# A float32 decoder layer on one core: the weight buffers moved to many residues modulo 256 bytes

## The chip, the cores and the metric

The kernel runs on one core of one Trainium2 chip. The metric is device time in microseconds (us), from launch to end, of the whole layer; lower is better. The core has a TensorE (PE: matmuls, with a separate record, PEld, for loading the stationary operand), a VectorE (DVE), a ScalarE (ACT), a GpSimd (POOL) and a SyncE (SP, which here only starts transfers). Its on-chip memory, SBUF, has 128 partitions; a tile takes the same range of bytes in each of them. "Address" below means that byte offset within a partition.

## The reference

One decoder layer over 512 tokens of width 1024, batch 1, in float32:

```python
x = x + 0.5 * swiglu(rms_norm(x, ffn1_norm), ffn1_gate, ffn1_up, ffn1_down)   # hidden width 2816
z = rms_norm(x, mix_norm) @ w_in                  # seven groups of 512 columns
y = concat(hgrn2_recurrence(z[0:4]), gated_short_convolution(z[4:7]))
x = x + y @ w_out
q = rms_norm(x, xattn_norm) @ w_q_mem             # 4 heads of 256
k, v = split(rms_norm(mem, mem_norm) @ w_kv_mem)  # 256 memory rows
x = x + softmax(q k^T / 16) v @ w_o_mem
x = x + 0.5 * swiglu(rms_norm(x, ffn2_norm), ffn2_gate, ffn2_up, ffn2_down)
out = rms_norm(x, final_norm)
```

## The kernel before

Features lie on partitions and tokens along the free axis, in 8 tiles of 128 features by 512 tokens, until the last projection, which puts tokens on partitions. To get float32 products out of TensorE's shorter format (float32r), every operand is split into a high and a low part of 12 bits each. A product then takes three matmuls, by `mm3`: high weight by high activation, high weight by low activation, low weight by high activation. Each loads 128x128 stationary values (512 bytes in each partition) and streams the other operand past them (512 columns, 2,048 bytes in each partition, nearly everywhere). There are 4,576 such float32r matmuls with 512 columns, 290 with 256, and 223 plain float32 ones.

Weights come in units of 128x1024 values. `weight_steps` gives a unit a tile `raw` (where the transfer lands), a tile `whi` and a tile `wlo`. ScalarE writes `whi` from `raw`, VectorE writes `wlo = raw - whi`, and TensorE then reads both in 24 matmuls. The pool `wpool` has three buffers each of `raw`, `whi` and `wlo`, used in turn. In the two feed-forward halves `extra[0]` names a pool with a fourth pair, used by each unit whose number is 3 modulo 4. The order of the work is the order of the code on each engine; a tile's next writer waits until its last reader is done.

Who is stationary differs. In the hidden layers, the first down projection, the mixer's projections, the queries, the memory's keys and the output projections, the weights are stationary and activations are streamed (`mm3`). In the values of the recurrence (`psv`), the memory's values (`psvm`) and the last down projection (`pso`), activations are stationary and weights are streamed.

The program's pools lay tiles one behind another, so each tile's address follows from the sizes ahead of it. In the built program before, the residues of the addresses modulo 256 are:

| tiles | residue |
|---|---|
| `x` (`xall`), its split tiles (`x_f1..`, `x_mx..`, `x_xa..`, `x_f2..`, `at..`), `raw`, all three `whi`, all three `wlo` | 160 |
| the fourth `whi` and `wlo`; the hidden activations `a_f1..`, `a_f2..`; everything in the mixer's pool (`qkh`, `kb`, `y..`, `memh`, `kh`, `q..`, `vh`, `pt..`) | 32 |
| `ones_r`, a matrix of ones | 224 |

All slices within these tiles start at multiples of 256 bytes. Take the distance of a pair as the address of the stationary operand being loaded, less that of the operand being streamed meanwhile, modulo 256. Of the 4,575 neighbouring pairs with 512 streamed columns, 2,927 have distance 0, 1,631 have distance 128, and 17 (with `ones_r` and the like) have 64 or 192. Distance 128 comes from a fourth unit against `x` tiles, or an ordinary unit against hidden activations or the mixer's tiles.

The stages in the profiled execution, by their first matmul: first hidden layer 6.3 us, first down projection 250.7 us, mixer 372.9 us, its output projection 557.7 us, memory's keys 603.7 us, output of the attention 719.6 us, last down projection 1009.1 us.

Of the kernel before, what the change touches and what calls it, by code (L numbers as in the profile page):

```python
# [8 lines left out]
F32 = mybir.dt.float32  # L9
F32R = mybir.dt.float32r  # L10
# [9 lines left out]
FF = 2816  # L20
KT = D // P          # 8 feature tiles
FT = FF // P         # 22 hidden tiles
NH = 4               # recurrence heads
TT = S // P          # 4 token tiles
MT = MEM // P        # 2 memory token tiles
MH = 4               # memory attention heads
EPS = 1e-6
# [3 lines left out]

# columns of the packed per-feature vectors
V_FFN1, V_MIX, V_XATT, V_MEM, V_FFN2, V_FIN = 0, 8, 16, 24, 32, 40
# [5 lines left out]
def decoder_layer(ctx: ExitStack, tc: tile.TileContext, xT, memT, vecs, masks, ident_d,  # L39
# [3 lines left out]
    xpool = ctx.enter_context(tc.tile_pool(name="xpool", bufs=KT))  # L43
    wpool = ctx.enter_context(tc.tile_pool(name="wpool", bufs=3))
    tmp = ctx.enter_context(tc.tile_pool(name="tmp", bufs=2))
    sm = ctx.enter_context(tc.tile_pool(name="sm", bufs=2))
# [7 lines left out]

    # ---------------------------------------------------------------- inputs
    inv_d = const.tile([P, 1], F32, name="inv_d")
# [7 lines left out]

    # the tensor engine's clock rises, and the activation tables come, while the first loads
    # are under way
    early = const.tile([P, 1], F32, name="early")
# [8 lines left out]
    msk = const.tile([P, len(LEVELS), 2, 64], U8, name="msk")  # L76
    lbv = const.tile([P, 2, NH], F32, name="lbv")
    xall = xpool.tile([P, KT, S], F32, tag="x", name="xall", bufs=1)
    x = [xall[:, k] for k in range(KT)]

    # ---------------------------------------------------------------- helpers
    n_unit = [0]
    extra = [None]          # a pool with room for a fourth block

    def weights(src, shape):
        """A block of weights, split into two parts of 12 bits each."""
        raw, hi, lo, load, split = weight_steps(src, shape)
        load(0, shape[0])
        split(0, shape[0])
        return hi, lo  # L90

    def weight_steps(src, shape):
        n = n_unit[0]
        n_unit[0] += 1
        raw = wpool.tile([P, 1024], F32, tag="raw", name=f"raw{n}")
        more = extra[0] is not None and n % 4 == 3
        hi, lo = (extra[0].tile([P, 1024], F32R, tag="x" + t, name=f"{t}{n}", bufs=1) if more else
                  wpool.tile([P, 1024], F32R, tag=t, name=f"{t}{n}") for t in ("whi", "wlo"))
        a, b = shape
        w = a * b  # L100

        def load(k0, k1, queue=nc.sync):
            queue.dma_start(raw[:, k0 * b:k1 * b], src[:, k0 * b:k1 * b])

        def split(k0, k1):
            c = slice(k0 * b, k1 * b)
            nc.scalar.activation(hi[:, c], raw[:, c], AF.Copy)  # L107
            nc.vector.tensor_tensor(lo[:, c], raw[:, c], r32(hi[:, c]), ALU.subtract)  # L108

        v = lambda t: t[:, :w].rearrange("p (a b) -> p a b", b=b)  # L110
        return raw, v(hi), v(lo), load, split

    def mm3(out, wh, wl, xh, xl, first, last):
        """out += (wh + wl).T @ (xh + xl), but for the product of the two low parts'
        2**-24."""
        nc.tensor.matmul(out, lhsT=wh, rhs=xh, start=first, stop=False)  # L116
        nc.tensor.matmul(out, lhsT=wh, rhs=xl, start=False, stop=False)  # L117
        nc.tensor.matmul(out, lhsT=wl, rhs=xh, start=False, stop=last)  # L118
# [6 lines left out]
    class Norm:  # L125
        """Sums of squares over features, tile by tile; then 1/rms by token in both layouts."""

# [12 lines left out]
        def tokens(self):  # L140
# [8 lines left out]
            nc.gpsimd.tensor_tensor(rst, rs, mhalf[:, :nt], ALU.pow)  # L149
            # 1/rms on a diagonal, in two parts of 12 bits: a sum over it fills all partitions  # L150
            hi = sm.tile([P, nt], F32R, tag="rsh", name=f"rsh_{self.name}")
# [23 lines left out]
    def prepare(gcol, name):  # L175
        """Scaled inputs of the next projections, from x's tiles."""
        norm = Norm(name, S)
        out = []

        def tile_done(k):  # L180
            hi, lo = new_split("x", xpool, f"x_{name}{k}")
            split_x(x[k], gcol + k, hi, lo)
            norm.add(x[k])
            out.append((hi, lo))

        return norm, out, tile_done
# [3 lines left out]

    # ---------------------------------------------------------------- SwiGLU halves
    def ffn_hidden(name, hp, xs, norm, wgu, first):
# [36 lines left out]

    # ---------------------------------------------------------------- first half  # L230
    norm, xs, _ = prepare(V_FFN1, "f1")
# [54 lines left out]

    # ---------------------------------------------------------------- mixer
    norm_a, xs_a, done_a = prepare(V_XATT, "xa")
    with tc.tile_pool(name="mix", bufs=8, reuse_waits="tile") as mp:
# [9 lines left out]

        # lower bound of the forget gate: the softmax over the two rows, its first row  # L300
        mx = sm.tile([P, NH], F32, tag="lb0", name="lbmx")
# [40 lines left out]

        # values, tokens on partitions
        v = mp.tile([P, TT, 512], F32, tag="b", name="v")
# [30 lines left out]
        def conv_u(j):  # L375
# [12 lines left out]
            for d in (1, 2):  # L388
# [3 lines left out]
                for n in range(d):  # L392
                    # steps at the edge between tiles: 2m -> 2m + 1, and 1 -> 2
                    tap(i, yt[:, :, 1, P - 1 - n:P - n], ut[:, :, 0, P - d + n:P - d + n + 1])
# [12 lines left out]

        # projections that keep the tensor engine busy between the steps of the recurrence
        fill = []
# [7 lines left out]

        # scores of the recurrence: s on partitions, t along the row; pairs within a tile of
        # 128 steps by halving, each pair through the step between its halves
        kmix = mp.tile([P, 2, 2 * NH, P], F32, tag="b", name="kmix")  # L420
# [8 lines left out]

        def pairs(a):            # [P, heads x tile pairs, tile of the pair, step]  # L430
            return a.rearrange("p n (m r t) -> p (n m) r t", r=2, t=P)
# [5 lines left out]
        kp, qp = pairs(kb), pairs(qa)  # L437
        tot, off = f, 0          # products of f over blocks of h steps: [P, heads, S // h]
        for li, h in enumerate(LEVELS):
            nb = P // (2 * h)  # L440
            # earlier halves of the first tile's blocks beside those of the second's, whose
            # steps run backwards
            km = kmix[:, li % 2]
# [3 lines left out]
            for half in range(2):  # L447
                ps = bank(f"ps_l{h}_{half}")
                for n in range(4):
                    g = 4 * half + n  # L450
                    # later halves of the first tile's blocks, then of the second's
                    qs = pick(qp[:, g], h, (P - h, 2), (2 * h, nb), (1, h))
                    nc.tensor.matmul(ps[:, n * P:(n + 1) * P], lhsT=km[:, g], rhs=qs, start=True, stop=True)
                pv = ps.rearrange("p (g r b c) -> p g r b c", g=4, r=2, c=h)
                for r in range(2):
# [3 lines left out]
                        pv[:, :, r])  # L459
            # blocks of 2h steps  # L460
            nb2 = S // (2 * h)
# [11 lines left out]
            filler(2 if li < 4 else 1)  # L473
        # tiles 0 -> 1 and 2 -> 3 of 128 steps
        so1 = mp.tile([P, NH, 2, P], F32, tag="b", name="so1")
# [13 lines left out]
        filler(2)  # L489
        # the first 256 steps -> the last 256  # L490
        so2 = mp.tile([P, NH, 2, 256], F32, tag="b", name="so2")
# [37 lines left out]
        for hh in range(NH):  # L529
# [9 lines left out]
            ys[hh] = (hi, lo)  # L539
        # the memory, split like x; its norm  # L540
        norm_k = Norm("mem", MEM)
# [27 lines left out]

        # ------------------------------------------------------------ attention to the memory  # L570
        norm_2, xs_2, done_2 = prepare(V_FFN2, "f2")
# [133 lines left out]

    # ---------------------------------------------------------------- second half, last norm
    with tc.tile_pool(name="hid2", bufs=FT, reuse_waits="tile") as hp:
        extra[0] = hp
        hid = ffn_hidden("f2", hp, xs_2, norm_2, w2, None)
        # from here on tokens lie on partitions  # L710
        for k in range(KT):
# [24 lines left out]
        def finish_tile(i):  # L736
# [11 lines left out]
            nc.vector.scalar_tensor_tensor(rs, ss[:, :1], EPS, ss[:, 1:], op0=ALU.add, op1=ALU.add)  # L748
            rst = sm.tile([P, 1], F32, tag="rstf", name=f"rstf{i}")
            nc.gpsimd.tensor_tensor(rst, rs, mhalf[:, :1], ALU.pow)  # L750
            return y, rst

        def store_tile(i, y, rst):
            # two engines share the products with 1/rms and the gain
            a, b = (1, 0) if i < TT - 1 else (0, 1)
# [21 lines left out]
def _tokens():  # L777
    """The order of the tokens on chip: every second tile of 128 from its end."""
    import numpy as np
# [5 lines left out]
def _layout(i):  # L785
# [3 lines left out]

    def cols(w, kt):       # [K, M] -> [M / 128, 128, K / 128 * 128]: lhsT blocks by output tile  # L790
        k, m = w.shape
# [55 lines left out]
```

## Time and profile before

| | |
|---|---|
| median of 2 runs | 1141.56 us (1141.05 to 1142.07) |
| span of the profiled execution, first to last instruction | 1138.9 us |
| TensorE busy | 1129.7 us |
| weight loads busy (beside the matmuls) | 937.9 us |
| VectorE busy | 572.6 us |
| ScalarE busy | 391.2 us |
| mean traffic to and from memory | 98 GB/s |

The profiled execution's time is given as its span alone; the median of the runs is 2.7 us above that, and what lies around the span (launch and end) is the same code in both kernels. A matmul's recorded duration (about 390 ns) is longer than the time from its start to the next one's start, because matmuls are pipelined: two are always under way. So durations of matmuls say little here; the time between starts is what adds up to the span.

### The profile page before, as it was taken

How to read it: one execution, taken by the hardware profiler on the slowest of the kernel's cores; microseconds unless marked ns; L12 is line 12 of the kernel's file. 1: busy time of each engine (PE TensorE's matmuls, PEld its weight loads, DVE VectorE, ACT ScalarE, POOL GpSimd, SP SyncE). 2: the span in 40 equal slices, each digit the busy share in tenths (PEclk: the TensorE clock that was granted, in tenths of full speed). 3: DMA queues.
4: the chain of work that ended last, by engine and by line, in shares of the span. 5: the costliest groups of instructions: out<-in, count | busy, mean ns of one | idle time of the engine just before them, and what ended most of it. 6: DMA issues, size and time to landing. Idle time of an engine off the chain costs nothing. (4 is left out here: it accounts for less than half of the span.)

```text
span 1138.9 us, 12928 instructions
## 1 busy us (share of the span) xinstructions
PE 1129.7 (99%) x5232; PEld 937.9 (82%) x5232; DVE 572.6 (50%) x829; ACT 391.2 (34%) x542; POOL 18.1 (2%) x21
## 2 busy tenths in 40 slices
PE   9999999999999999999999999999999999999997
PEld 7888888888888888888889888888888888888885
DVE  6644444443333466885677566464544444432224
ACT  6423332222222344324455346343323223331123
POOL 0000000000000000000100000000000000000002
PEclk9999999999999999999999999999999999999999
DMA  6333222332332222222134323223222232232211
GB/s 232 121 104 99 93 93 93 102 91 86 101 92 102 74 93 84 84 74 93 56 129 138 122 75 129 64 92 123 93 93 93 96 107 94 93 102 101 93 56 74
DMA packets 33195, 112.02 MB, mean 98 GB/s; under 512 B 3968, under 2 KB 4736, under 8 KB 33136
## 3 DMA queue, kind: packets, MB, share of 16 engines
q1 hardware_dynamic: 30960, 108.02, 28.9%
q10 hardware_dynamic: 2016, 2.66, 0.7%
q8 instruction: 41, 0.67, 0.2%
q0 software_dynamic: 160, 0.52, 0.1%
q14 instruction: 18, 0.15, 0.0%
HBM read 109.09 MB, written 2.10 MB: 98 GB/s over the span
## 5 line engine op out<-in xcount | busy, mean ns | idle before, releaser
L107 ACT ACTIVATE whi<-raw 128x1024 fp32r<-128x1024 f32 (+4 forms) x208 | 213.0, 1028 | 632.9 <-PE ps_f L117 277.7
L108 DVE TENSOR_TENSOR wlo<-raw,whi 128x1024 fp32r<-128x1024 f32 (+4 forms) x208 | 245.1, 1182 | 194.7 <-ACT whi L107 194.4
L210 DVE TENSOR_TENSOR u_f<-ps_f,rsb_f 128x512 f32<-128x512 f32 x44 | 30.4, 690 | 128.6 <-PE ps_f L118 128.6
L207 DVE TENSOR_TENSOR t_f<-ps_f,rsb_f 128x512 f32<-128x512 f32 x44 | 30.4, 690 | 79.4 <-PE ps_f L118 79.4
L211 DVE TENSOR_TENSOR u_f<-u_f,t_f 128x512 f32<-128x512 f32 x44 | 30.3, 692 | 4.0
L208 ACT ACTIVATE t_f<-t_f 128x512 f32<-128x512 f32 x44 | 27.7, 630 | 1.6 <-DVE t_f L207 1.1
L116 PE MATMUL psk<-memh,whi 128*128 128x256 f32 x64 | 18.1, 283 | 0.0
L117 PE MATMUL psk<-meml,whi 128*128 128x256 f32 x64 | 18.0, 281 | 0.0
L118 PE MATMUL psk<-memh,wlo 128*128 128x256 f32 x64 | 18.0, 281 | 0.0
L117 PE MATMUL ps_f<-x_f12l,whi 128*128 128x512 f32 x44 | 17.4, 395 | 0.3 <-DVE x_f12l L123 0.3
L118 PE MATMUL ps_f<-x_f10h,wlo 128*128 128x512 f32 x44 | 17.3, 393 | 0.2 <-DVE wlo L108 0.2
L116 PE MATMUL ps_f<-x_f11h,whi 128*128 128x512 f32 x44 | 17.3, 392 | 0.2 <-ACT whi L107 0.2
L116 PE MATMUL ps_f<-x_f20h,whi 128*128 128x512 f32 x44 | 17.4, 395 | 0.0
L189 DVE SCALAR_TENSOR_TENSOR xall<-psd_f,xall 128x512 f32<-128x512 f32 x8 | 5.5, 692 | 23.5 <-PE psd_f L118 23.5
L116 PE MATMUL ps_f<-x_f12h,whi 128*128 128x512 f32 x44 | 17.3, 393 | 0.0
L118 PE MATMUL ps_f<-x_f17h,wlo 128*128 128x512 f32 x44 | 17.3, 393 | 0.0
L117 PE MATMUL ps_f<-x_f22l,whi 128*128 128x512 f32 x44 | 17.3, 393 | 0.0
L118 PE MATMUL ps_f<-x_f24h,wlo 128*128 128x512 f32 x44 | 17.3, 393 | 0.0
L116 PE MATMUL ps_f<-x_f27h,whi 128*128 128x512 f32 x44 | 17.3, 393 | 0.0
L118 PE MATMUL ps_f<-x_f27h,wlo 128*128 128x512 f32 x44 | 17.3, 393 | 0.0
L118 PE MATMUL ps_f<-x_f14h,wlo 128*128 128x512 f32 x44 | 17.3, 393 | 0.0
L116 PE MATMUL ps_f<-x_f17h,whi 128*128 128x512 f32 x44 | 17.3, 393 | 0.0
(1021 smaller groups left out, 3071.9 us busy)
## 6 DMA issues: line engine op xcount, KB each, us to landing
raw<-in_w SPq DMA_DIRECT2D x85, 512.0 KB, 3.5
raw<-in_w_in SPq DMA_DIRECT2D x24, 512.0 KB, 3.5
raw<-in_w2d SPq DMA_DIRECT2D x22, 512.0 KB, 3.5
raw<-in_w1d SPq DMA_DIRECT2D x16, 448.0 KB, 3.3
raw<-in_w1d SPq DMA_DIRECT2D x8, 512.0 KB, 3.6
raw<-in_w_out SPq DMA_DIRECT2D x8, 512.0 KB, 3.5
raw<-in_w_k SPq DMA_DIRECT2D x8, 512.0 KB, 3.5
raw<-in_w_q SPq DMA_DIRECT2D x8, 512.0 KB, 3.5
```

Source lines behind the costliest of these rows:

```text
L107: nc.scalar.activation(hi[:, c], raw[:, c], AF.Copy)
L108: nc.vector.tensor_tensor(lo[:, c], raw[:, c], r32(hi[:, c]), ALU.subtract)
L116: nc.tensor.matmul(out, lhsT=wh, rhs=xh, start=first, stop=False)
L117: nc.tensor.matmul(out, lhsT=wh, rhs=xl, start=False, stop=False)
L118: nc.tensor.matmul(out, lhsT=wl, rhs=xh, start=False, stop=last)
L189: nc.vector.scalar_tensor_tensor(x[k], ps, scale, x[k], op0=ALU.mult, op1=ALU.add)
L207: nc.vector.tensor_tensor(t, ps[0], bc, ALU.mult)
L208: nc.scalar.activation(t, t, AF.Silu)
L210: nc.vector.tensor_tensor(u, ps[1], bc, ALU.mult)
L211: nc.vector.tensor_tensor(u, u, t, ALU.mult)
```

## The change

No instruction is added, removed or moved: the two built programs have the same instructions in the same order on every engine. What differs is where tiles lie, and how the fourth pair is held.

```diff
+    WPAD = {"whi": 16, "wlo": 8}
...
-    lbv = const.tile([P, 2, NH], F32, name="lbv")
+    lbv_w = const.tile([P, 32], F32, name="lbv")
+    lbv = lbv_w[:, :2 * NH].rearrange("p (r h) -> p r h", r=2)
...
         raw = wpool.tile([P, 1024], F32, tag="raw", name=f"raw{n}")
         more = extra[0] is not None and n % 4 == 3
-        hi, lo = (extra[0].tile([P, 1024], F32R, tag="x" + t, name=f"{t}{n}", bufs=1) if more else
-                  wpool.tile([P, 1024], F32R, tag=t, name=f"{t}{n}") for t in ("whi", "wlo"))
+        if more:
+            both = extra[0].tile([P, 2048 + 128], F32R, tag="xw", name=f"w{n}", bufs=1)
+            hi, lo = both[:, 4:4 + 1024], both[:, 1090:1090 + 1024]
+        else:
+            hi, lo = (wpool.tile([P, 1024 + WPAD[t]], F32R, tag=t, name=f"{t}{n}")[:, :1024]
+                      for t in ("whi", "wlo"))
...
-            rst = sm.tile([P, 1], F32, tag="rstf", name=f"rstf{i}")
+            rst = sm.tile([P, 24], F32, tag="rstf", name=f"rstf{i}")[:, :1]
```

The rest of the diff takes comments out. The padding of `whi` (64 bytes each) and `wlo` (32 bytes each) gives each buffer a residue of its own; the padding of `lbv` and `rstf` moves what lies behind them. The residues modulo 256 in the changed program:

| tiles | residue |
|---|---|
| `x`, its split tiles, `raw` | 0 |
| the three `whi` | 0, 64, 128 |
| the three `wlo` | 192, 224, 0 |
| the fourth pair, now in one tile | high part 48, low part 40 |
| hidden activations, everything in the mixer's pool | 32 |
| `ones_r` | 224 |

The high and low buffers come round together: high 0 with low 192, high 64 with low 224, high 128 with low 0. Of the same 4,575 pairs, the distance (to the nearer side, 0 to 128) is now 0 in 937, 8 in 84, 16 in 168, 32 in 917, 40 in 176, 48 in 352, 64 in 1,013, 96 in 357 and 128 in 571. From one pair to the next the distance stays the same nearly always before (it changes 109 times); now it changes 3,079 times, since high and low parts alternate.

Because the fourth pair is one tile, ScalarE's next write to its high part waits for the last reader of either part, one matmul later than before; four of VectorE's writes to its low part lose their own wait for TensorE.

## The prediction, made before the changed kernel ran

> **What bounds the kernel now.** I read the page first, then the listing in order of time at five places. The page:
>
> ```profile
> PE 1129.7 (99%) x5232; PEld 937.9 (82%) x5232; DVE 572.6 (50%) x829; ACT 391.2 (34%) x542; POOL 18.1 (2%) x21
> PEclk9999999999999999999999999999999999999999
> L107 ACT ACTIVATE whi<-raw 128x1024 fp32r<-128x1024 f32 (+4 forms) x208 | 213.0, 1028 | 632.9 <-PE ps_f L117 277.7
> L108 DVE TENSOR_TENSOR wlo<-raw,whi 128x1024 fp32r<-128x1024 f32 (+4 forms) x208 | 245.1, 1182 | 194.7 <-ACT whi L107 194.4
> raw<-in_w SPq DMA_DIRECT2D x85, 512.0 KB, 3.5
> ```
>
> TensorE is occupied in 1129.7 of 1138.9 us at a full clock. The two engines that prepare weights wait for it, not it for them: ScalarE stood still 277.7 us ahead of `whi` until a matmul of the hidden layers released a buffer. So the time is the sum of the intervals between starts of matmuls, and the question is what one interval costs at each distance between the streamed operand and the weights loaded meanwhile. The trace before holds both of the old kernel's distances, so I can price them. Distance 0, in the queries (`psq`; start, duration, engine, line):
>
> ```profile
> 636.63 0.39 PE L116 MATMUL psq<-x_xa5h,whi 128*128 128x512 f32 x1
> 636.86 0.39 PE L117 MATMUL psq<-x_xa5l,whi 128*128 128x512 f32 x1
> ...
> 639.12 0.39 PE L118 MATMUL psq<-x_xa0h,wlo 128*128 128x512 f32 x1
> 639.35 0.39 PE L116 MATMUL psq<-x_xa1h,whi 128*128 128x512 f32 x1
> ```
>
> From the first to the last are 12 intervals in 2.72 us: 226.7 ns each, and steady. Distance 128, in the first hidden layer: unit 15, the fourth pair, is loaded against the same kind of activations, and then unit 16 at distance 0 follows:
>
> ```profile
> 91.40 0.40 PE L118 MATMUL ps_f<-x_f17h,wlo 128*128 128x512 f32 x1
> 91.63 0.40 PE L116 MATMUL ps_f<-x_f10h,whi 128*128 128x512 f32 x1
> ...
> 96.75 0.40 PE L117 MATMUL ps_f<-x_f17l,whi 128*128 128x512 f32 x1
> 96.98 0.40 PE L118 MATMUL ps_f<-x_f17h,wlo 128*128 128x512 f32 x1
> 97.22 0.39 PE L116 MATMUL ps_f<-x_f10h,whi 128*128 128x512 f32 x1
> ...
> 97.91 0.39 PE L116 MATMUL ps_f<-x_f11h,whi 128*128 128x512 f32 x1
> ...
> 102.67 0.39 PE L116 MATMUL ps_f<-x_f10h,whi 128*128 128x512 f32 x1
> 102.69 1.06 ACT L107 ACTIVATE whi<-raw 128x1024 fp32r<-128x1024 f32 x1 [3.12 <-PE ps_f L117]
> 103.79 1.23 DVE L108 TENSOR_TENSOR wlo<-raw,whi 128x1024 fp32r<-128x1024 f32 x1 [0.23 <-ACT whi L107]
> ```
>
> From 91.40 to 96.98 are 24 intervals in 5.58 us: 232.5 ns each, 5.8 ns dearer than distance 0, with the same instructions on the same data shapes. Back at distance 0 the price does not fall at once: 96.98 to 97.91 are four intervals in 0.93 us (232.5 ns), and only 97.91 to 102.67, 21 intervals in 4.76 us, has 226.7 again. So the interval depends on the distance, and it has a memory of some four matmuls. A third distance, 192, stands once, where a matrix of ones is stationary:
>
> ```profile
> 439.63 0.39 PE L426 MATMUL ps_s<-qkh,ones_r 128*128 128x512 f32 x1
> ...
> 441.23 0.40 PE L426 MATMUL ps_s<-qkl,ones_r 128*128 128x512 f32 x1
> ```
>
> Seven intervals in 1.60 us: 228.6 ns, between the other two. With 256 columns streamed the distance hardly matters, nor in the same direction:
>
> ```profile
> 604.74 0.28 PE L116 MATMUL psk<-memh,whi 128*128 128x256 f32 x1
> ...
> 606.40 0.28 PE L118 MATMUL psk<-memh,wlo 128*128 128x256 f32 x1
> ...
> 650.75 0.28 PE L615 MATMUL pssc<-kl,q1h 128*128 128x256 f32 x1
> ...
> 652.19 0.28 PE L615 MATMUL pssc<-kl,q1h 128*128 128x256 f32 x1
> ```
>
> `psk` at distance 128: 14 intervals in 1.66 us, 118.6 ns; `pssc` at distance 0: 12 in 1.44 us, 120.0 ns. Also, 256 columns more cost 226.7 - 120.0 = 106.7 ns at distance 0, so 512 columns alone are 213.4 ns, and an interval at distance 0 has 13.3 ns over that, one at distance 128 has 19.1 ns. These few per cent are all that the change can touch.
>
> **The change part by part.** *No instruction added or removed*, so nothing is summed there.
>
> *The matmuls with 512 columns.* Priced by these rows, the old kernel's 4,575 intervals are 2,927 x 226.7 + 1,631 x 232.5 + 17 x 228.6 ns = 663.6 + 379.2 + 3.9 = 1046.7 us; the remaining 92.2 us of the span are matmuls of other shapes, the start, the end and gaps, which the change leaves. For the distances that no row shows I draw a line between 0 and 128: 226.7 + 5.8 x distance/128. At 64 it gives 229.6, against 228.6 measured at 192, which is as far from 0 on the other side. With the counts of the changed program (937 at 0, 84 at 8, 168 at 16, 917 at 32, 176 at 40, 352 at 48, 1,013 at 64, 357 at 96, 571 at 128) the mean distance is 49.4 bytes against 45.9 before, so the sum is 1047.5 us: 0.9 us more. What was cheap gets dearer (nearly two thirds of the pairs at 0 leave it), what was dear gets cheaper (two thirds of those at 128 leave it), and the two cancel.
>
> *The lost steadiness.* Before, the distance changes 109 times; after, 3,079 times, two in three matmuls, because high and low parts have different residues. If no interval ever settled, all would cost what the four behind a change cost or what distance 128 costs, 232.5 ns: 4,575 x 232.5 = 1063.7 us, 17.0 us more than now. If all settled at the price of distance 0 they would be 1037.2 us, 9.5 us less. I take the line's value with little on top, +1.5 us, because in the rows the extra price shows on a return to distance 0, and with three buffers such returns last one or two matmuls before the distance changes again; both ends go into the range.
>
> *Matmuls with 256 columns and float32 ones:* by the two rows at 256 columns the price moves by 1.4 ns or less either way on 290 matmuls, under 0.4 us.
>
> *ScalarE, VectorE and the transfers* now use other addresses. A unit's split takes 1.06 and 1.23 us in the rows above, while TensorE needs 24 x 226.7 ns = 5.4 us for a unit; a landing takes 3.5 us and is issued units ahead. Even at double their durations they stay under it: 0. If that cover went, TensorE would show waits for `whi`, of which the page has none worth naming.
>
> *One tile for the fourth pair:* ScalarE's write waits one matmul (0.23 us) longer. It writes that buffer some three units of 5.4 us before TensorE reads it, so 0. Nothing else is queued behind it but the next unit's split, with the same slack.
>
> Sum: 1141.56 + 0.9 + 0.6 = about 1143 us (on the span, 1140.4).
>
> **A rule against the rows.** The row is the 5.8 ns between distances. The Trainium skill ("TensorE: Matmul & The Clock Gate", the step-by-step part on loading the stationary operand) says that TensorE has two independent read ports, so that loading the next weights takes no read bandwidth from the running matmul. By that rule the distance could not matter. The trace disagrees, 226.7 against 232.5 ns, and the measurement decides. The same page (section "Back-to-back issue gap") puts an isolated matmul of 512 columns at 512/2.4 + 2.5 = 215.8 ns; an estimate from it for all 4,575 would be 987 us, 59 us less than now. No row here shows an interval that short held.
>
> **The rivals.**
>
> 1. *Some of the new distances avoid the conflict.* At distance 0, 13.3 ns stand over the bare columns, and nothing shows that 0 is the cheapest distance; at 256 columns 128 was even cheaper than 0. If the mixture kept half of the 13.3 ns, an interval would be 220 ns: 4,575 x 220.0 = 1006.5 us, 40 us less, 1101 us in all. It decides (2% faster, 22.8 us) from a mean of 223.8 ns. Against it: distances 0, 128 and 192 all stand at or above 226.7, and a mixture has to be good in most of its parts.
>
> 2. *Each change of distance costs anew; slower.* The step from 128 to 0 gave a first interval of 0.24 us (96.98 to 97.22), the dearest there. Taken as 236 ns for the 3,079 intervals behind a change, and 231 for the other 1,496, the sum is 726.6 + 345.6 = 1072.2 us, 25.5 us more: 1167 us. It decides from a mean of 233.8 ns, above even the steady price of 128. For it: the memory of four matmuls, which the new order never lets run out. Against it: the first interval after going from 0 to 128 (91.40 to 91.63, 0.23 us) is no dearer than 128 itself.
>
> 3. *The change does nothing,* because what sets the price is something else that goes with the stages (which buffers, which banks of results), and the distance only happens to go with it: 1141.6 us. Against it, `ps_f` has both prices within one stage, unit after unit. The rule of two independent ports would give the same time.
>
> **How the numbers follow.** The sum's own case, 55%: 1143 us, with its own range of 1132 (all at 226.7 ns) to 1158 us (all at 232.5). Rival 3, 12%: 1141.6. Rival 1, 21%: around 1101 and up to 1118. Rival 2, 12%: from 1164, around 1167. Within 2% of before, about what a measurement of this kernel can tell from no change, thus lies 0.67; faster by more 0.21; slower by more 0.12. The range that holds the time 8 times in 10 reaches into rival 1 as far as 1106, leaving a tenth below, and up to 1163, leaving a tenth above.
>
> **What would show it.** In the changed profile the intervals of 512-column matmuls should scatter between some 224 and 241 ns without settling, with means of 228 to 231 ns in every stage. The steady 226.7 of `psq` should be gone, unit 15 of the hidden layer should be cheaper than 232.5, and `psd_f` and `pso` cheaper than before while `ps_f`, `psz`, `psq` and `pswo` get dearer. ScalarE's and VectorE's splits should keep 1.06 and 1.2 us. The prediction is wrong if any large group holds under 224 ns (rival 1), if means stand over 233.8 ns (rival 2), or if TensorE starts to wait for `whi` or `wlo`.

## The result, and the profile after

The changed kernel takes 1154.57 us (1154.55 to 1154.58, 2 runs) against 1141.56: 13.0 us more, a ratio of 1.011 with a 95% interval of 1.009 to 1.013. It is slower by about 1%, inside the 2% that was named beforehand as no clear change. Its profiled execution spans 1152.8 us, 13.9 more than the one before.

The page of the changed kernel, the lines on the engines and on the two steps that split weights (their line numbers moved by 7):

```profile
PE 1142.7 (99%) x5232; PEld 939.0 (81%) x5232; DVE 573.2 (50%) x829; ACT 391.5 (34%) x542; POOL 18.0 (2%) x21
...
L114 ACT ACTIVATE whi<-raw 128x1024 fp32r<-128x1024 f32 (+4 forms) x175 | 178.5, 1023 | 523.4 <-PE ps_f L124 204.6
L115 DVE TENSOR_TENSOR wlo<-raw,whi 128x1024 fp32r<-128x1024 f32 (+4 forms) x175 | 205.7, 1178 | 164.3 <-ACT whi L114 163.7
```

TensorE is occupied for 13.0 us longer, with as many instructions; VectorE's, ScalarE's and GpSimd's busy times stay within 0.6 us. ScalarE still waits for TensorE, and a split takes what it took. TensorE's own waits for weight parts (`whi`, `wlo`, `w`) come to 1.3 us, against 0.4 before. (The counts at `whi` and `wlo` fell because the fourth pair is now called `w`.) So nearly all of the time went into the intervals between matmuls. The cheapest way to see it is to count the matmuls that TensorE starts in a fixed stretch. First the kernel before (stretch in us, its length, TensorE's busy time and matmuls, clock, share of the DMA engines, GB/s): the first hidden layer, the first down projection, the attention's output projection, the last down projection:

```profile
60.00:210.00 150.00, 150.00 (x658) 1.00 0.29 95
270.00:370.00 100.00, 100.00 (x434) 1.00 0.32 98
730.00:755.00 25.00, 25.00 (x112) 1.00 0.26 88
1040.00:1120.00 80.00, 80.00 (x346) 1.00 0.22 73
```

The same four stretches of the changed kernel:

```profile
60.00:210.00 150.00, 150.00 (x648) 1.00 0.29 95
270.00:370.00 100.00, 100.00 (x431) 1.00 0.31 95
730.00:755.00 25.00, 25.00 (x109) 1.00 0.23 75
1040.00:1120.00 80.00, 80.00 (x346) 1.00 0.26 86
```

Ten matmuls fewer in 150 us of the hidden layer, where three units in four had been at distance 0; three fewer of 112 in the output projection, where all had been at 0; hardly a change in the two down projections, where most had been at 128. A unit of the hidden layer shows how the rhythm is lost. Here the high part lies at distance 128, the low part at 0:

```profile
60.09 0.40 PE L123 MATMUL ps_f<-x_f10h,whi 128*128 128x512 f32 x1
60.33 0.40 PE L124 MATMUL ps_f<-x_f10l,whi 128*128 128x512 f32 x1
60.57 0.39 PE L125 MATMUL ps_f<-x_f10h,wlo 128*128 128x512 f32 x1
60.80 0.39 PE L123 MATMUL ps_f<-x_f11h,whi 128*128 128x512 f32 x1
...
65.47 0.39 PE L125 MATMUL ps_f<-x_f17h,wlo 128*128 128x512 f32 x1
65.70 0.39 PE L123 MATMUL ps_f<-x_f10h,whi 128*128 128x512 f32 x1
```

24 intervals in 5.61 us are 233.8 ns, a little more than a whole unit at 128 took before (232.5), although a third of its loads are at distance 0.

Mean interval by stage, worked out from all starts of 512-column matmuls in the two traces (intervals over 300 ns, which hold waits, are left out of the means; the difference is that of the means times the number of matmuls):

| stage (matmuls) | before, ns | after, ns | difference, us |
|---|---|---|---|
| both hidden layers, `ps_f` (2,112) | 228.5 | 232.2 | 7.8 |
| mixer's projections, `psz` (576) | 227.4 | 232.1 | 2.7 |
| queries and output, `psq`, `pswo` (384) | 226.9 | 231.9 | 1.9 |
| first down projection, `psd_f` (528) | 231.4 | 232.9 | 0.8 |
| recurrence's values, `psv` (96) | 226.7 | 230.7 | 0.4 |
| `psw`, `psvm`, last down projection `pso` (816) | 232.2 | 232.1 | -0.1 |

The sum, 13.5 us, is the whole loss of the span but 0.4 us. It falls on the stages that had been at distance 0; those that had mostly been at 128 hardly changed.

### The profile page after: what moved, and what is told of

Same layout as the page of the kernel before. It is cut to its first block, busy times and chain, and to the rows that moved or that the text cites. A ratio compares the mean times of both kernels' runs of the same rounds, so it can differ in the third digit from the quotient of the medians.

```text
span 1152.8 us, 12928 instructions
## 1 busy us (share of the span) xinstructions
PE 1142.7 (99%) x5232; PEld 939.0 (81%) x5232; DVE 573.2 (50%) x829; ACT 391.5 (34%) x542; POOL 18.0 (2%) x21
## 5 line engine op out<-in xcount | busy, mean ns | idle before, releaser
L114 ACT ACTIVATE whi<-raw 128x1024 fp32r<-128x1024 f32 (+4 forms) x175 | 178.5, 1023 | 523.4 <-PE ps_f L124 204.6
L115 DVE TENSOR_TENSOR wlo<-raw,whi 128x1024 fp32r<-128x1024 f32 (+4 forms) x175 | 205.7, 1178 | 164.3 <-ACT whi L114 163.7
L114 ACT ACTIVATE w<-raw 128x1024 fp32r<-128x1024 f32 (+1 forms) x33 | 34.7, 1051 | 127.8 <-PE ps_f L125 84.1
L115 DVE TENSOR_TENSOR w<-raw,w 128x1024 fp32r<-128x1024 f32 (+1 forms) x33 | 39.8, 1206 | 32.6 <-ACT w L114 32.6
L196 DVE SCALAR_TENSOR_TENSOR xall<-pswo,xall 128x512 f32<-128x512 f32 x8 | 5.5, 691 | 21.6 <-PE pswo L125 21.6
L460 PEld LDWEIGHTS ps_l<-qa,kmix 128*128 128x128 f32 x112 | 13.6, 191 | 1.0 <-ACT kmix L452 0.5
L460 PE MATMUL ps_l<-qa,kmix 128*128 128x128 f32 x112 | 13.8, 276 | 0.0
L125 PE MATMUL ps_f<-x_f15h,wlo 128*128 128x512 f32 x33 | 13.2, 399 | 0.0
L125 PE MATMUL ps_f<-x_f11h,wlo 128*128 128x512 f32 x33 | 13.2, 399 | 0.0
L125 PE MATMUL ps_f<-x_f23h,wlo 128*128 128x512 f32 x33 | 13.1, 398 | 0.0
```

What stands on the lines that cost most here:

```text
L196: nc.vector.scalar_tensor_tensor(x[k], ps, scale, x[k], op0=ALU.mult, op1=ALU.add)
```

## The experiments

Two theories were to be told apart. By the first, each distance has a price of its own, and the changed kernel only holds dearer ones. By the second, matmuls that keep one distance settle into a cheap rhythm whatever the distance is, and the price is that of leaving it: every change of distance costs anew. A third, that distance has nothing to do with it, was tried along with them. The first kernels all come from the kernel before; a pad tile ahead of the weight buffers sets their residue, and another puts all activations at one residue:

```diff
+        if n == 0 and DH:
+            wpool.tile([P, DH // 4], F32, tag="pad", name="pad", bufs=1)
...
+            hi, lo = (extra[0].tile([P, 1088], F32R, tag="x" + t, name=f"{t}{n}", bufs=1)[:, o:o + 1024]
+                      for t, o in (("whi", FH // 4), ("wlo", FL // 4)))
...
+                self.acc = sm.tile([P, self.n + (HPAD if self.n == MEM else 0)], F32, tag=f"acc{self.n}",
+                                   name=f"acc_{self.name}", bufs=1)[:, :self.n]
```

**Everything at distance 0** (`DH, FH, FL, HPAD = 0, 0, 0, 32`).

> All weight buffers, the fourth pair and all activations at one residue: distance 0 in 4,558 of the 4,575 pairs, hardly any change of distance (13). Both theories (a price that goes with the distance; a price for each change of distance): 226.7 ns per interval, the 1,631 pairs that were at 128 gain 5.8 ns each, 9.5 us: 1132 us. Rival, that the price goes with the stage or the buffers and not with the distance: no change, 1141.6 us, and the fourth units and the first down projection stay at 232.5 ns.

Measured: 1131.49 us against 1142.29 for the kernel before on the same chip, a ratio of 0.990 (0.989 to 0.992). The four stretches:

```profile
60.00:210.00 150.00, 150.00 (x664) 1.00 0.27 95
270.00:370.00 100.00, 100.00 (x443) 1.00 0.32 99
730.00:755.00 25.00, 25.00 (x112) 1.00 0.26 95
1040.00:1120.00 80.00, 80.00 (x355) 1.00 0.21 74
```

The two down projections now start 443 and 355 matmuls where they had 434 and 346, and the hidden layer 664 for 658. The mean over 4,526 intervals at distance 0 is 226.9 ns. So the price goes with the distance and not with the stage, and this version beats both kernels.

**One constant distance of 64 bytes** (`DH, FH, FL, HPAD = 64, 64, 64, 16`).

> One distance for all weights, 64 bytes (3,784 pairs; 192 in the 718 where weights are streamed), 47 changes of distance. Theory of the price by distance alone: the 234.3 ns that pairs at 64 behind pairs at 64 take in the changed kernel, and 231.7 at 192, make 3,784 x 234.3 + 718 x 231.7 = 1053 us, with the 73 others 1069.5, 22.9 us more than the 1046.7 before: 1164 us. Theory of the price for changes: a constant distance settles, at the 228.6 to 229.6 ns of the prediction's line, 1032 + 17 = 1049 us in all: 1144 us.

Measured: 1156.26 us, 1.012 of before (1.010 to 1.014), between the two forecasts.

```profile
60.00:210.00 150.00, 150.00 (x645) 1.00 0.26 93
270.00:370.00 100.00, 100.00 (x431) 1.00 0.32 98
730.00:755.00 25.00, 25.00 (x109) 1.00 0.18 64
1040.00:1120.00 80.00, 80.00 (x351) 1.00 0.26 92
```

A constant distance did not settle at a low price: 3,755 intervals at 64 take 233.3 ns on average, in the stages with stationary weights alike (233.3 in `ps_f`, `psd_f`, `psz`, `psw` and `pswo`, 233.4 in `psq`). The stages that stream weights have 192 here, and take 228.9 ns. This is against the theory that only changes cost.

**High parts at 0, low parts at 128** (`GAP, FL = 128, 128`, where `GAP` is a pad between the high and the low buffers, so that only these two distances occur, alternating).

> High parts at distance 0, low parts at 128, everywhere: only the two distances of the kernel before (3,047 and 1,511 pairs, nearly its mix), but the distance now changes 3,022 times. Price by distance alone: 3,047 x 226.7 + 1,511 x 232.5 ns, 4.5 us less than before... less the same mix at 1,137 us. Price for changes: no interval settles, 232.5 ns or more for all, 1,063 us instead of 1,047: 1158 us or more.

Measured: 1151.70 us, 1.008 of before (1.007 to 1.010). The stretches in the hidden layer and the first down projection:

```profile
60.00:210.00 150.00, 150.00 (x651) 1.00 0.28 97
270.00:370.00 100.00, 100.00 (x434) 1.00 0.31 96
```

The 1,137 us of the expectation left out the 17 pairs at other distances; with their 3.9 us, a price by distance alone makes 1141 us. The run speaks for the theory of changes: nearly the mix of the kernel before (3,047 pairs at 0, 1,511 at 128), but pairs at 0 now take 230.7 ns on average instead of 226.9, and those at 128 still 232.7. Alternating makes the cheap distance dear. It came out lower than the 1158 us of that theory, since only a pair at 0 right behind one at 128 takes 233.3 ns; one behind another pair at 0 takes 228.1. So both theories hold in part.

**More constant distances.** 32, 192, 96 and 128 bytes with the same pads; for 16, 48 and 8 bytes both parts of a unit were put in one tile at an offset:

```diff
+        both = (extra[0].tile([P, 2112], F32R, tag="xw", name=f"w{n}", bufs=1) if more else
+                wpool.tile([P, 2112], F32R, tag="w", name=f"w{n}"))
+        hi, lo = both[:, OH:OH + 1024], both[:, 1024 + OL:2048 + OL]
```

> As d64, with 32 bytes (224 where weights are streamed). Price by distance alone: the 233.3 ns that pairs at 32 behind pairs at 32 take in the changed kernel (231.1 at 224): about 15 us more in all, 1160 us. Price for changes: settled near the line's 228.2 ns, 1143 us.

> One distance for all weights, 192 bytes (64 in the 729 pairs where weights are streamed). If the price goes with the signed distance and nothing else, the 228.9 ns that 192 took in the last projection of the run at 64, and 233.3 at 64: 3,773 x 2.2 + 729 x 6.6 ns over the 1131.5 of the run at 0, 13 us: 1145 us. Rival, that in that projection something else than the distance made it cheap (streamed weights, stationary activations): 233 ns here too, 4,502 x 6.5 = 29 us: 1161 us.

> One distance, 96 bytes (160 where weights are streamed). A steady price by distance: the 231.6 ns of pairs at 96 behind 96 in the changed kernel, and 234.6 at 160: 3,773 x 4.9 + 718 x 7.9 = 24 us over the run at 0: 1156 us. Rival, that 226.7 holds at every constant distance but a few: 1132 us; the runs at 32 and 64 speak against it.

> One distance of 128 bytes. The kernel before has it in 1,631 pairs at 232.5 to 233.3 ns; at that price for all, 4,502 x 5.8 to 6.6 ns over the run at 0: 1158 to 1161 us. Rival: with everything else equal it settles lower, as nothing ever switches back to 0.

> One distance of 16 bytes (240 where weights are streamed), half of the smallest so far. If memory is read in pieces of 32 bytes and only the piece counts, 16 is as good as 0 (226.7 ns, 1132 us). If the distance counts to the byte, as the 233.0 ns of 16 behind 16 in the changed kernel's first down projection say, 3,774 x 6.3 + 718 x 4.8 = 27 us more: 1159 us.

> One distance of 48 bytes (208 where weights are streamed), that of the fourth pair in the changed kernel's hidden layers, without its partner at 40. A steady price by distance like that of 32 and 64, 233.3 ns: 3,774 x 6.6 + 718 x about 4 = 28 us over the run at 0: 1159 us. If the fourth pair's 232.5 and 231.5 ns came from the change between 48 and 40 alone, it settles near 227: 1133 us.

> One distance of 8 bytes (248 where weights are streamed). If any distance but 0 loses the steady interval, 1155 to 1160 us as with 16 to 48. If pieces of 16 bytes count, 8 is like 0: 1132 us. The run at 16 gave both 1140 and 1155 us in its executions, so here too the times may lie apart; each execution would then show stages at 226.7 and stages at 233.3 ns.

| distance | us (runs) | ratio to before, 95% interval | mean interval where weights are stationary, ns | with weights streamed (distance), ns |
|---|---|---|---|---|
| 0 | 1131.49 (4) | 0.989 to 0.992 | 226.9 | 226.7 (0) |
| 8 | 1149.98 (4) | 1.005 to 1.008 | 230.7 | 233.3 (248) |
| 16 | 1154.46 (8) | 1.003 to 1.012 | 232.1 | 231.6 (240) |
| 32 | 1159.88 (2) | 1.013 to 1.017 | 233.3 | 233.3 (224) |
| 48 | 1159.75 (2) | 1.013 to 1.019 | 233.3 | 233.3 (208) |
| 64 | 1156.26 (4) | 1.010 to 1.014 | 233.3 | 228.9 (192) |
| 96 | 1163.73 (2) | 1.016 to 1.022 | 234.3 | 233.3 (160) |
| 128 | 1157.22 (2) | 1.011 to 1.015 | 232.7 | 233.3 in `pso` (128) |
| 192 | 1150.48 (2) | 1.005 to 1.011 | 230.7 | 233.3 (64) |

The runs at 32, 48 and 128 bytes came as the price by distance had it, within 1 us. At 96 the price was sized too low (1156 us forecast, from 231.6 ns); pairs at 96 right behind pairs at 96 take 234.7 ns in the changed kernel's trace, near the 234.3 of this run. The run at 192 fell between its two forecasts, because the price isn't one per distance: the queries and the output projection took 228.9 ns there, the first down projection 233.3. At 8 and 16 bytes the time lay between the two forecasts. Neither is as good as 0, so it isn't a piece of 16 or 32 bytes that counts. At 16 bytes one execution holds both rhythms at one distance, in the hidden layer and in the output projection:

```profile
60.00:210.00 150.00, 150.00 (x645) 1.00 0.26 93
...
730.00:755.00 25.00, 25.00 (x112) 1.00 0.22 75
```

645 in 150 us is what the run at 64 has; 112 in 25 us is what distance 0 has. Its eight executions lay between 1140.32 and 1155.77 us, while those of every other kernel made for these experiments lie within 3 us of one another. So the addresses alone do not fix the time there. That it is again the rhythm of whole stages that differs from one execution to the next is likely but not shown, since one execution alone has a trace.

**The padding of the three buffers alone undone**, in the changed kernel:

```diff
-    WPAD = {"whi": 16, "wlo": 8}
+    WPAD = {"whi": 0, "wlo": 0}
```

> The changed kernel with the padding of whi and wlo alone undone: 3,778 pairs at distance 0, 660 with the fourth pair at 8 or 16 (or 248 and 240), 585 changes of distance; all residues are 0 where the run at distance 0 had 160. If what counts is the distance, 3,778 pairs take 226.7 ns and the 660 others 230 to 233.3: 2 to 5 us over the run at 0, 1134 to 1136 us, so the padding of the three buffers makes the whole loss. If residue 160 itself was what made the run at 0 fast, or if the merged fourth tile costs, it stays near 1150.

Measured: 1135.85 us, 0.994 of before (0.993 to 0.996): 18.7 us less than the changed kernel.

```profile
60.00:210.00 150.00, 150.00 (x659) 1.00 0.27 95
270.00:370.00 100.00, 100.00 (x440) 1.00 0.31 98
730.00:755.00 25.00, 25.00 (x112) 1.00 0.30 106
1040.00:1120.00 80.00, 80.00 (x351) 1.00 0.21 73
```

Without the padding, everything but the fourth pair lies at residue 0, hidden activations and mixer's tiles too (with it they move to 32). 3,752 intervals at distance 0 take 227.1 ns, and those of the fourth pair at 8 and 16 bytes 229.9 and 233.1. So the padding, with what it moves behind it, is the loss; one merged tile for the fourth pair costs nothing that shows; and distance 0 is about as good at residue 0 as at 160.

**Many distances, but both parts of a unit at the same one**, in the changed kernel:

```diff
-    WPAD = {"whi": 16, "wlo": 8}
+    WPAD = {"whi": 16, "wlo": 16}
...
-            hi, lo = (wpool.tile([P, 1024 + WPAD[t]], F32R, tag=t, name=f"{t}{n}")[:, :1024]
-                      for t in ("whi", "wlo"))
+            hi = wpool.tile([P, 1024 + WPAD["whi"]], F32R, tag="whi", name=f"whi{n}")[:, :1024]
+            if n == 0:
+                wpool.tile([P, 16], F32, tag="pad", name="pad", bufs=1)
+            lo = wpool.tile([P, 1024 + WPAD["wlo"]], F32R, tag="wlo", name=f"wlo{n}")[:, :1024]
+            if n == 0:
+                wpool.tile([P, 24], F32, tag="pad2", name="pad2", bufs=1)
```

> The changed kernel with many distances kept, but the high and low part of a unit at the same one (0, 64 and 128 in turn, the fourth 48): 282 changes of distance instead of 3,079, 953 pairs at 0 instead of 937. If it is the change of distance that costs, the 0 units settle at 226.7 (in the changed kernel their pairs take 231.2): 4 us less, and the 64 and 128 units go to their steady 233.3 and 232.5: 1148 to 1151 us. If only the distances count, the same 1154.6 within 1 us.

Measured: 1153.80 us (1153.49 to 1156.45), 1.010 of before (1.008 to 1.012): 0.8 us less than the changed kernel, which isn't a difference beyond the runs' own spread, and what the theory of distances alone had forecast. The profiled execution, from which the means come, is the longest of the four. The pairs at 0 did settle, at 227.8 ns (231.2 in the changed kernel). But the pairs at 224 bytes, which alternation had made cheap (230.2 ns there), are 233.0 here, and those at 48 went from 232.6 to 233.3. What is won at 0 is lost elsewhere. The distances aren't quite the same as in the changed kernel; at the prices of the table above they would cost 0.6 us more. By that estimate alternation as such has 1.4 us of the changed kernel's time, less than the spread of these four runs, so a share of its own is not shown. What costs is that so few pairs are left at 0.

## Why the prediction came out as it did

**The forecast** of no clear change held, and the time lies within the stated range, 1106 to 1163 us. But it is 11.6 us above the sum's 1143 and near the upper end of the sum's own case: the range was wide enough, the sum was not right.

**What bounds the kernel** was read rightly: the sum of the intervals between matmuls is the time, and the changed profile shows no new wait beyond 0.9 us for weights.

**That the price goes with the distance** held: the run at 0 against the run at 64 has the same instructions in the same order and differs by 24.8 us. By the Trainium skill's rule ("TensorE: Matmul & The Clock Gate", "Step-by-step: what each phase is for") that two independent read ports let the next load run without taking read bandwidth from the running matmul, the two runs would take the same time; the measurement decides against it here as in the prediction.

**The prices of the distances that no row showed** is the step that failed. The prediction drew a line from 226.7 ns at 0 to 232.5 at 128, which made 228.2 at 32, 228.9 at 48 and 229.6 at 64. The runs gave 233.3 at all three. There is no slope: the price stands at its full height by 32 bytes, and 8 bytes cost more than half of it. With the means of the runs at one distance (the table; 233.3 taken at 40), the changed program's counts give 1059.7 us and the old one's 1047.5: 12.3 us more, where the line gave 0.9. The measured difference is 13.0 us, so the mis-sized line is nearly all of the error. The row at 192, 228.6 ns, was the wrong support for it: it was taken for a mirror of 64, but 192 is a cheaper place than 64 (its run's mean is 230.7, and 228.9 in the queries), and seven intervals were few. (The mean distance after the change is 50.0 bytes by the prediction's own counts, not 49.4; its sum of 1047.5 us is right.)

**The lost steadiness** was given 0.6 us by choice. Shown: alternating between 0 and 128 costs (pairs at 0 at 230.7 instead of 226.9 ns). In the changed kernel, though, keeping both parts of a unit together won only 0.8 us, as alternation makes other pairs cheaper. Its share is thus 1.4 us by estimate and the runs cannot tell it from nothing; that the choice was near it is luck.

**The upper end** of the sum's own case, all intervals at 232.5 ns, 1158 us, was near: the mean after is 232.2 over the stages of the table.

**Costed at nothing or nearly**: splits, transfers, matmuls of other shapes and the merged fourth tile. The page bears out the first (1.02 and 1.18 us a split as before), the run without padding the last; the 0.4 us that the table of stages leaves over bounds the rest.

**The rivals.** That some new distance is cheaper than 0 falls: of the eight other constant distances that were run none has a lower price than 0 with 512 columns. That each change costs anew, at 1167 us, is bounded by the alternating run. That distance is only an accompaniment falls with the run at 0.

**The signs foretold**: the steady 226.7 of the queries went (232.0 there), the intervals scattered (223 to 242 ns in the hidden layers), unit 15 got cheaper (231.0 ns), and hidden layers, mixer and output projection got dearer as said. The two down projections were to get cheaper, and did not: the first went from 231.4 to 232.9 ns and the last stayed at 231.8, since their new distances (8 to 96 off the hidden activations) are hardly cheaper than 128. And the means came out at 231.8 to 232.9 ns in every stage of the table but the recurrence's values (230.7), above the 228 to 231 that were foretold: the line again.

## What to carry to other kernels

Where TensorE is the bound, loads new stationary values for each matmul and streams 512 columns, look at the time between starts by the residue of the two operands' addresses modulo 256 bytes. Here a distance of exactly 0 was the only one that held the shortest interval in all stages, 2.7% under that at 32 to 64 bytes, and putting every pool at the same residue gained 1% over a kernel that had it for two thirds of its matmuls. Measure at the number of columns that is streamed: with 256, in the memory's keys (`psk`), it was the other way round, 119.8 ns at 0 and 115.6 at 64 bytes. A price seen at two points is not a line: an alignment effect may stand at full height one step away.

## What the runs showed that was not expected

- At a constant distance the intervals settle into a pattern that repeats. In the first down projection all are 226 or 227 ns at 0; at 64 they are 231 and 236 ns in turn; at 8 five repeat (230, 231, 229, 230, 234), at 96 and at 128 seven; in the output projection at 192 three repeat (226, 229, 232). Each pattern adds up to a whole multiple of 6.667 ns, within 0.02 ns on average: 34 for the one, 70 for the two, 173 for the five, 246 and 244 for the seven, 103 for the three. So the means 226.7, 233.3, 230.7, 234.3, 232.4 and 228.9 are steps, not points of a slope. What stands behind 6.667 ns, and why equal residues are the cheap ones, stays open; no run here shows it.
- At one distance a stage can hold either price, and two runs of the same kernel at 16 bytes can differ by 15 us.
- 8 bytes between the operands, two elements, cost 3.8 ns of 226.9 per matmul.
